# The first branch product of a token mixer in seven block products, kept PSUM banks, and a later quarter of the modulation

## The chip, the cores and the metric

The kernel runs on one core of a Trainium2 chip. TensorE (PE in the views) multiplies, VectorE (DVE) and ScalarE (ACT) work on tiles, GpSimd (POOL) here mostly issues transfers from DRAM to DRAM and writes zeros, and SyncE (SP) issues most loads. Every engine runs its own instructions in order and waits on semaphores for the others; transfers go through 16 DMA engines. The metric is the device time of one execution in microseconds, the median of several.

## The reference

One layer of a diffusion backbone on 512 tokens of width 1024. What matters here, cut from the reference:

```python
z = h @ w_in
u, vs, q, r, ga, gb, k, v, lr = _split(z, IN_SPLITS)
a = _spatial_gating(gelu(u), gelu(vs), ...)
o, s_f, s_b = _gla_bidir(...)
ob = o.astype(h.dtype) * jax.nn.silu(r)
merged = jax.nn.sigmoid(ga) * (a @ w_br_a) + jax.nn.sigmoid(gb) * (ob @ w_br_b)
return merged @ w_o, s_f, s_b
...
x = x + g1x * y_x
hx2 = _modulate(_rms_norm(x, norm2_g[l]), sh2x, sc2x)
x = x + g2x * _conv_ffn(hx2, rows, w_up, conv_w, conv_b, w_down)
```

`r`, `ga`, `gb`, `a`, `ob` and `merged` are 512 x 1024, the three weights behind them 1024 x 1024. `g1`, `sh2`, `sc2` and `g2` are quarters of `silu(c) @ w_ada + b_ada`.

## The kernel before

Each float32 operand is split into a rounded part and a rest (`wh` and `wl` for weights, `ah` and `al` and the like for activations), and a product is three matmuls: high by high, high by low, low by high. A matmul takes 128 x 128 stationary values and 512 columns.

**The weight stream.** `specs` lists all weight blocks in the order of their use, 512 KB each. `stream_load` lets SyncE load a block into one of four `raw` buffers; `stream_split` makes `wh` by a ScalarE cast (L245) and `wl` by a VectorE subtraction (L246), in one of five buffers each; `weights()` hands out the next block and moves the stream on.

**Seven products.** r, ga and gb are computed by `gate` (L1333 is its matmul): the 2 x 2 blocks of a product take seven block products instead of eight, a11, p1, s2, a21, s3, q4 and a22. Each is 24 matmuls into a pair of PSUM banks (two weight blocks, two row halves). Three pairs are used, X, Z and Y; some products go on adding to a bank, some outputs are put together by `taken` (a ScalarE copy out of a bank, L1316) and `combine` (a VectorE sum, L1321). The sums of weight quarters that it needs are built in DRAM: `sums_build` copies a quarter into a `sum` tile and adds others to it by accumulating transfers on POOL's queue. `gate_sums` is a generator that the code moves on one step at a time, in `weights()` from position SUMS0 on and in `hook`; each transfer is tied to the instruction written before it. The sums of activations (`hx_sums`) are made once.

**r.** `r_gate` takes a sigmoid, multiplies by the normalised `o` (L1300) and then by r (L1302). `ob_turn` transposes the result (L1309) and spills it to DRAM.

**The branches.** a @ w_br_a and ob @ w_br_b and merged @ w_o are done by `wide_tm` (L398): eight blocks of weights, 192 matmuls: first four output tiles side by side, then four one after another. The tiles of `a` and `ob` lie in DRAM and are brought back by `restores`, eight tiles each, split by ScalarE and VectorE (L372, L373). `sga` and `sgb` are the gates' sigmoids; the results are multiplied in.

**The modulation.** `ada2` is background work, a step for each `tick`: a load of 256 KB (`wa`), and a VectorE multiply and add (L1194) a few steps later (ADA2); at its end the sum is split and two small matmuls with ones (L1204, L1205) bring it to all rows. Before, g1, sh and sc, and g2 all run from r to w_o, by the numbers in `ticks` and in the steps of the branches. Behind it comes the up projection, with one pair of feature blocks after another (48 matmuls each), a convolution on VectorE, and `prep`, which makes operands of down; then down, by 7 block products again.

The order of the instructions of one engine comes from a scheduler, which works on the order in the code, and from `in_order`, which fixes a piece of it.

## Time and profile before

| | us |
|---|---|
| median of 3 runs | 916.73 (916.11 to 918.77) |
| the profiled execution | 916.65 |
| its span | 914.9 |
| TensorE, VectorE, ScalarE busy | 899.8, 706.9, 449.6 |
| r gate, on TensorE | from 300.9 |
| ga, gb | from 339, from 379.3 |
| a @ w_br_a | 420.2 to 463.7 |
| ob @ w_br_b, merged @ w_o | from 463.7, from 512.3 |
| up, down | 572.9 to 801.4, from 801.4 |

The span runs from the first to the last instruction that the profiler recorded; the device time has a little around it. Times in the views are counted from the span's start. TensorE's clock was full (0.998 of it). The views quoted below give busy time and mean duration of groups of instructions, the chain of waits that ended last, and the busy time of each engine in stretches of time.

### The profile page before, as it was taken

To read this page: it belongs to the slowest core of one execution; us is meant where nothing else is said; L and a number is where in the kernel's file an instruction comes from. 1 tells how busy PE (TensorE), PEld (TensorE's weight loads), DVE (VectorE), ACT (ScalarE), POOL (GpSimd) and SP (SyncE) were. 2 spreads that over 40 slices of the span, in tenths; PEclk is the share of its full clock that TensorE was granted. 3 is DMA by queue.
4 is the path that set the end of the run, shared out by engine and by line. 5 is a ranking of instruction groups with operands and counts; after the bars stand their busy time and mean duration, and the time that the engine had idled before them with its cause. 6 is when DMAs were issued, how large, how long until landed. Compare 5 with 4: busy or idle time off the path is not lost.

```text
span 914.9 us, 12458 instructions
## 1 busy us (share of the span) xinstructions
PE 899.8 (98%) x4500; PEld 750.1 (82%) x4500; DVE 706.9 (77%) x1183; ACT 449.6 (49%) x741; POOL 86.3 (9%) x138
## 2 busy tenths in 40 slices
PE   7999999999999999999999999999999999999996
PEld 5678888888888888888888889888888888888885
DVE  6468687779776698569797657898777778998956
ACT  6256455647543556755241537443333433467643
POOL 1310112122121100000000000011111000000000
PEclk9999999999999999999999999999999999999999
DMA  9970758698799759789877660788998632355552
GB/s 285 331 251 24 237 156 162 221 293 167 200 238 253 245 190 304 243 257 401 292 284 253 235 230 25 242 209 166 210 186 200 143 92 95 118 172 191 164 159 92
DMA packets 149819, 187.99 MB, mean 205 GB/s; under 512 B 8777, under 2 KB 85909, under 8 KB 149757
## 3 DMA queue, kind: packets, MB, share of 16 engines
q1 hardware_dynamic: 127981, 133.45, 45.5%
q0 software_dynamic: 19936, 50.56, 23.5%
q10 hardware_dynamic: 1840, 3.18, 0.9%
q8 instruction: 35, 0.57, 0.2%
q14 instruction: 27, 0.22, 0.1%
HBM read 178.77 MB, written 54.53 MB: 255 GB/s over the span
## 4 chain that ended last, share of the span: by engine, by line
PE 92%; DMA 2%; DVE 2%; ACT 1%; SPq 1%; issue 0%; ACTq 0%; DVEq 0%
PE mm L380 32%; PE mm L398 19%; PE mm L1333 9%; PE gl L1716 9%; PE gl L1333 4%; PE gl L910 3%; PE gl L398 2%; PE mm L674 2%; PE mm L1716 1%; PE mm L1072 1%; PE gl L674 1%; PE mm L1022 1%; DMA raw<-in_w_in_dram 1%; DMA wa<-in_w_ada_dram 1%; PE gl L945 1%; PE gl L1229 1%
## 5 line engine op out<-in xcount | busy, mean ns | idle before, releaser
L245 ACT CAST wh<-raw 128x1024 fp32r<-128x1024 f32 x172 | 180.3, 1053 | 216.7 <-PE mm L380 87.1
L246 DVE TENSOR_TENSOR wl<-raw,wh 128x1024 fp32r<-128x1024 f32 x172 | 208.8, 1220 | 78.9 <-ACT wh L245 75.9
L380 PE MATMUL mm<-h2l,wh 128*128 128x512 f32 (+1 forms) x344 | 133.0, 387 | 0.0
L380 PE MATMUL mm<-h2h,wh 128*128 128x512 f32 (+1 forms) x344 | 133.0, 387 | 0.0
L380 PE MATMUL mm<-h2h,wl 128*128 128x512 f32 (+1 forms) x344 | 133.0, 387 | 0.0
L1563 DVE SCALAR_TENSOR_TENSOR cacc<-ca,ccol,cacc 128x441 f32<-128x441 f32 (+2 forms) x176 | 121.8, 695 | 4.1
L380 PEld LDWEIGHTS mm<-h2h,wl 128*128 128x128 f32 x344 | 64.6, 188 | 13.2
L380 PEld LDWEIGHTS mm<-h2l,wh 128*128 128x128 f32 x344 | 64.6, 188 | 13.1
L380 PEld LDWEIGHTS mm<-h2h,wh 128*128 128x128 f32 x344 | 64.6, 188 | 12.9
L1194 DVE SCALAR_TENSOR_TENSOR acc<-wa,cs,acc 128x512 f32<-128x512 f32 x64 | 46.1, 746 | 4.6 <-DMA wa<-in_w_ada_dram 4.6
L1716 PE MATMUL gl<-wh,dah 128*128 128x512 f32 x120 | 46.7, 389 | 0.0
L1716 PE MATMUL gl<-wl,dah 128*128 128x512 f32 x120 | 46.7, 389 | 0.0
L1716 PE MATMUL gl<-wh,dal 128*128 128x512 f32 x120 | 46.7, 389 | 0.0
L380 PE MATMUL mm<-hxh,wh 128*128 128x512 f32 x104 | 41.3, 397 | 0.0
L380 PE MATMUL mm<-hxl,wh 128*128 128x512 f32 x104 | 40.6, 390 | 0.0
L380 PE MATMUL mm<-hxh,wl 128*128 128x512 f32 x104 | 40.5, 390 | 0.0
L1564 ACT ACTIVATE cacc<-cacc 128x512 f32<-128x512 f32 x22 | 13.9, 632 | 49.4 <-DVE cacc L1563 49.3
L398 PE MATMUL mm<-wh,hxh 128*128 128x512 f32 x88 | 34.9, 396 | 0.9 <-ACT kq L1037 0.9
L398 PE MATMUL mm<-wl,hxh 128*128 128x512 f32 x88 | 34.3, 390 | 0.0
L398 PE MATMUL mm<-wh,hxl 128*128 128x512 f32 x88 | 34.3, 390 | 0.0
L1333 PE MATMUL gl<-wh,xs 128*128 128x512 f32 x96 | 30.8, 392 | 0.0
L1333 PE MATMUL mm<-wh,xs 128*128 128x512 f32 x96 | 30.6, 390 | 0.0
(474 smaller groups left out, 2011.8 us busy)
## 6 DMA issues: line engine op xcount, KB each, us to landing
wa<-in_w_ada_dram SPq DMA_DIRECT2D x96, 256.0 KB, 5.7
raw<-in_w_in_dram SPq DMA_DIRECT2D x46, 512.0 KB, 4.5
raw<-sum SPq DMA_DIRECT2D x44, 512.0 KB, 3.7
raw<-in_ffn_w_up_dram SPq DMA_DIRECT2D x44, 512.0 KB, 5.1
sum<-in_w_in_dram POOLq DMA_DIRECT2D x36, 512.0 KB, 6.9
sum<-in_ffn_w_down_dram POOLq DMA_DIRECT2D x30, 512.0 KB, 6.7
sum<-sum POOLq DMA_DIRECT2D x22, 512.0 KB, 7.7
raw<-in_ffn_w_down_dram SPq DMA_DIRECT2D x17, 512.0 KB, 4.2
```

Of the source, the lines that this page charges most:

```text
L245: A.copy(wh, raw)
L246: V.tensor_tensor(wl, raw, wh.bitcast(F32), op=ALU.subtract)
L380: T.matmul(ps, a[:, k, :], b[:, c0:c0 + n], start=(k == 0 and i == 0), stop=(k == KT - 1 and i == 2))
L398: T.matmul(ps, a[:, t * P:(t + 1) * P], b[:, k % 2, :], start=(k == 0 and i == 0), stop=(k == KT - 1 and i == 2))
L674: T.matmul(fps[i], a, b, start=(k == 0 and z == 0), stop=(k == KT - 1 and z == 2))
L910: T.matmul(ps, p_, q_, start=(start and z == 0), stop=(stop and z == 2))
L945: T.matmul(sc[:, i * P:(i + 1) * P], S_["k"][d][:, i, :], S_["q"][d][:, i, :], start=True, stop=True)
L1194: V.scalar_tensor_tensor(acc[i], coming.pop(0), cs[:, k, 0:1], acc[i], op0=ALU.mult, op1=ALU.add)
L1333: T.matmul(banks[t], a(kk, t), w[:, kk, :], start=(first and b == 0 and kk == 0 and i == 0), stop=(b == 1 and kk == 1 and i == 2), skip_gr ...
L1563: V.scalar_tensor_tensor(o, a_[:, r0 + dy:r1 + dy, c0 + dx:c1 + dx], wcol(tap), o, op0=ALU.mult, op1=ALU.add)
L1564: A.activation(acc, acc, AF.Gelu)
L1716: T.matmul(ps, a, w[:, kk, c0:c0 + n_], start=(first and kk == 0 and i == 0), stop=(last and kk == 1 and i == 2), skip_group_check=True)
```

## The change

In words: a @ w_br_a is computed by `gate` too, so `a` comes back from DRAM in quarters (16 loads of 128 KB) and `a_prep` makes its block sums and splits during gb. w_br_a's blocks come as 14 in the stream, after those of gb, and its eight sums are built in DRAM like the gates' (16 more transfers), with more steps of `gate_sums` in two loops further ahead. r takes one Silu on ScalarE in place of a sigmoid and a multiply. The three pairs of banks are allocated once and kept over r, ga, gb and the new gate, X and Y changing places; from the second gate on, the first product is copied by ScalarE from its bank into the bank of a21, which adds to it. The steps of `ada2` are dealt out anew: fewer in gb, g2 not before the fifth feature block of up, with its loads 12 steps ahead; sh and sc have theirs 6 ahead. In down two groups are put behind others.

```diff
 EARLY = 8
-SUMS0 = 78
+SUMS0 = 84
 ADA2 = 3
+SHSC = 6
+WT = (1, 1)
+RAW = 4
...
     R_AT = len(specs)
-    for w_ in (w_br_a, w_br_b, w_o):
+    for w_ in (w_br_b, w_o):
         for hf in range(2):
...
     gate_weights = [(quarters(wi, c0), sum_tiles(2)) for c0 in (O_R, O_GA, O_GB)]
+    gate_weights.append((quarters(w_br_a[0], 0), sum_tiles(2)))
     down_specs, specs = specs, []
...
         prod_k(kps, k1, hx, k, 0, S)
+        if k % 2:
+            next(building[1][1])
     kxs[1] = heap([P, S], s="kq")
...
         hooked[0] += 1
-        if (hooked[0] % 2 or pos[2] < 10) and 2 < pos[2] < R_AT:
+        if hooked[0] % 2 and 2 < pos[2] < R_AT:
             next(building[1][1], None)
...
                          stop=(k == KT - 1 and i == 2))
+            if k % 2:
+                next(building[1][1])
         v_out(4 + t, ps)
...
-    def ada2(*kinds):
+    def ada2(*kinds, ahead=ADA2):
         todo = [(kind, j) for kind in kinds for j in range(2)]
...
         coming, steps_ = [], [(k, i) for k in range(KT) for i in range(len(todo))]
-        for n in range(len(steps_) + ADA2):
+        for n in range(len(steps_) + ahead):
             if n < len(steps_):
...
                 coming.append(w_)
-            if n >= ADA2:
-                k, i = steps_[n - ADA2]
+            if n >= ahead:
+                k, i = steps_[n - ahead]
                 V.scalar_tensor_tensor(acc[i], coming.pop(0), cs[:, k, 0:1], acc[i], op0=ALU.mult, op1=ALU.add)
...
-    def r_sum(name):
-        for b in range(2):
-            yield [lambda kk, t, z=z: z[:, kk, t * P:(t + 1) * P] for z in hx_sums[name, b]]
-
-    def r_quad(i, hf):
+    def of_sums(found):
+        return lambda name: ([lambda kk, t, z=z: z[:, kk, t * P:(t + 1) * P] for z in found(name, b)] for b in range(2))
+
+    def r_quad(name):
+        i, hf = int(name[1]) - 1, int(name[2]) - 1
         for b in range(2):
...
-    def r_gate(hf, t, src):
+    r_sum = of_sums(lambda name, b: hx_sums[name, b])
+
+    def r_silu(src):
         z = late([P, 512], s="obt")
-        A.activation(z, src, AF.Sigmoid)
+        A.activation(z, src, AF.Silu)
+        return z
+
+    def r_gate(hf, t, z):
         for hh in range(2):
...
                                    op0=ALU.mult, op1=ALU.mult)
-        V.tensor_tensor(z, src, z, op=ALU.mult)
         ob_t[hf, t] = z
...
-    def gate(out, pool, at={}, mids=late):
-
-        X, Z, Y = ([bank() for _ in range(2)] for bank in (mm, gl, mm))
+    banks = []
+
+    def gate(out, pool, at={}, mids=late, quad=r_quad, sum_=r_sum):
+
+        fresh = not banks
+        banks.extend([bank() for _ in range(2)] for bank in (mm, gl, mm) if fresh)
+        X, Z, Y = banks
+        banks.reverse()
         later = lambda i: at.get(i, lambda: None)()
-        gate_product(X, r_quad(0, 0), True)
-        m1 = [taken(z, mids) for z in X]
+        gate_product(X, quad("a11"), True)
+        if fresh:
+            m1 = [taken(z, mids) for z in X]
+        else:
+            for t in range(2):
+                A.copy(Y[t], X[t])
         later(0)
-        gate_product(Z, r_sum("p1"), True)
+        gate_product(Z, sum_("p1"), True)
         m5 = [taken(z, mids) for z in Z]
         later(1)
-        gate_product(X, r_sum("s2"))
+        gate_product(X, sum_("s2"))
         u2 = [taken(z, mids) for z in X]
         later(2)
-        gate_product(Y, r_quad(1, 0), True)
+        gate_product(Y, quad("a21"), fresh)
         for t in range(2):
-            out(0, t, combine(Y[t], m1[t], ALU.add, pool))
+            out(0, t, combine(Y[t], m1[t], ALU.add, pool) if fresh else Y[t])
         later(3)
-        gate_product(X, r_sum("s3"))
+        gate_product(X, sum_("s3"))
         for t in range(2):
...
         later(4)
-        gate_product(Z, r_sum("q4"))
+        gate_product(Z, sum_("q4"))
         for t in range(2):
...
         later(5)
-        gate_product(X, r_quad(1, 1))
+        gate_product(X, quad("a22"))
         later(6)
...
     def r_out(hf, t, src):
+        z = r_silu(src)
         if (hf, t) in ((0, 0), (0, 1), (1, 2), (1, 3)):
-            r_gate(hf, t, src)
+            r_gate(hf, t, z)
         else:
-            pending.append((hf, t, src))
-
-    bg += [ada2("g1"), ada2("sh", "sc"), ada2("g2")]
-    ticks = [0] * 2 + [1] * 6 + [0] * 10 + [1] * 10 + [1, 2] * 7
+            pending.append((hf, t, z))
+
+    bg += [ada2("g1"), ada2("sh", "sc", ahead=SHSC)]
+    ticks = [0] * 2 + [1] * 6 + [0] * 6 + [0, 0] + [1] * 12 + [0, 1] * 7 + [1, 1, 2] * 5
     gate(r_out, heap, mids=heap)
...
         def out(hf, t, src):
-            z = src if hf or t < 2 else heap([P, 512], s=name)
+            z = src if hf else heap([P, 512], s=name)
             A.activation(z, src, AF.Sigmoid)
...
     gate(squash(sga, "sga"), heap, {i: lambda i=i: ga_step(i) for i in range(7)}, heap)
-    a_act, a_step = restores(a_kept, "a")
+    found = {}
+
+    def a_prep():
+        tiles = {}
+        for i, hf in ((0, 0), (0, 1), (1, 1), (1, 0)):
+            for b in range(2):
+                t_ = heap([P, 2, 256], s="aq")
+                for kk in range(2):
+                    dma(t_[:, kk], a_kept[4 * b + 2 * i + kk][:, hf * 256:(hf + 1) * 256])
+                tiles[f"a{i + 1}{hf + 1}", b] = t_
+            yield
+
+        def kept(name, b, src):
+            hi, lo = heap([P, 2, 256], F32R, s="ah"), late([P, 2, 256], F32R, s="al")
+            A.copy(hi, src)
+            V.tensor_tensor(lo, src, hi.bitcast(F32), op=ALU.subtract)
+            found[name, b] = hi, lo
+
+        for name in ("a11", "p1", "s2", "a21", "s3", "q4", "a22"):
+            for b in range(2):
+                a11, a12, a21, a22 = (tiles["a" + z, b] for z in ("11", "12", "21", "22"))
+                if name == "p1":
+                    p1 = tiles["p1", b] = heap([P, 2, 256], s="aq")
+                    V.tensor_tensor(p1, a12, a22, op=ALU.subtract)
+                    kept(name, b, p1)
+                elif name == "s2":
+                    p1 = tiles["p1", b]
+                    V.tensor_tensor(p1, p1, a11, op=ALU.subtract)
+                    kept(name, b, p1)
+                elif name == "s3":
+                    V.tensor_tensor(a12, a11, a12, op=ALU.subtract)
+                    kept(name, b, a12)
+                elif name == "q4":
+                    V.tensor_tensor(a21, a21, tiles["p1", b], op=ALU.add)
+                    kept(name, b, a21)
+                else:
+                    kept(name, b, tiles[name, b])
+                yield
+
+    a_steps = a_prep()
+
+    def a_step(n):
+        for _ in range(n):
+            next(a_steps, None)
+
     ob, ob_step = restores(ob_kept, "ob")
-    gate(squash(sgb_t, "sgb"), heap, {i: a_step if i > 2 else lambda i=i: ob_turn(i + 5) for i in range(7)})
-
-
-    def bra_done(hf, t, ps):
-        V.tensor_tensor(sga[hf, t], ps, sga[hf, t], op=ALU.mult)
-
-    count = [0]
-
-    def bra_step():
-        count[0] += 1
-        a_step()
-        if count[0] > 11:
+
+    def gb_step(i):
+        if i < 3:
+            ob_turn(i + 5)
+        a_step((4, 2, 2, 2, 2, 2, 2)[i])
+
+    gate(squash(sgb_t, "sgb"), heap, {i: lambda i=i: gb_step(i) for i in range(7)})
+
+    def bra_out(hf, t, src):
+        V.tensor_tensor(sga[hf, t], src, sga[hf, t], op=ALU.mult)
+
+    def bra_step(i):
+        a_step((2, 0, 0, 0, 0, 0, 0)[i])
+        if i > 3:
             ob_step()
-        tick(1 + count[0] % 2)
-
-    wide_tm(a_act, bra_done, bra_step)
+
+    a_sum = of_sums(lambda name, b: found.pop((name, b)))
+    gate(bra_out, heap, {i: lambda i=i: bra_step(i) for i in range(7)}, late, a_sum, a_sum)
     mg = []
...
         ob_step()
-        tick(2)
+        tick((1 + (len(ob) >= 8)))
...
     wide_tm(ob, brb_done, brb_step, {(2 + j // 2, 4 * (j % 2)): lambda j=j: mg_turn(j) for j in range(4)})
-    drain()
     am2 = const([P, 8], "am2")
-    V.tensor_scalar(am2, cols["sc"], 1.0, None, op0=ALU.add)
-    V.tensor_tensor(am2, am2, n2g, op=ALU.mult)
-    bm2 = cols["sh"]
+
+    def ada2_end():
+        drain()
+        V.tensor_scalar(am2, cols["sc"], 1.0, None, op0=ALU.add)
+        V.tensor_tensor(am2, am2, n2g, op=ALU.mult)
...
-    hooks += [(mg_turn, 4), (mg_turn, 5), (mg_turn, 6), (mg_turn, 7)] + [(lambda: None,)] * 4 + [(crow_turn, 0), (crow_turn, 1)]
+    hooks += [(lambda j=j: (mg_turn(j), tick(WT[0])),) for j in range(4, 8)] + [(tick, WT[1])] * 4 + [(ada2_end,)]
+    hooks += [(crow_turn, 0), (crow_turn, 1)]
     wide_tm(mg, wo_done, hook, {(2, 6): turn_first})
...
         conv_part(f, pa, pv)
+        if f == 4:
+            bg.append(ada2("g2", ahead=12))
+        last = max(i for i, z in enumerate(traced()) if z.engine == V.engine)
+        tick(4 if f < 7 else 2)
+        in_order(last, V.engine)
         prep(min(EARLY, BLOCKS, (f + 1) // 4) if f < 4 * BLOCKS - 2 else min(EARLY, f - 4 * BLOCKS + 3 + BLOCKS))
...
+    def behind_last(f, *engines):
+        ends = [max(i for i, z in enumerate(traced()) if z.engine == e.engine) for e in engines]
+        f()
+        for e, i in zip(engines, ends):
+            in_order(i, e.engine)
+
     def product_in(ps, t, c0, n_, z, first, last):
...
     def operands():
-        prep(n[0] + LEAD)
+        behind_last(lambda: prep(n[0] + LEAD), A, V)
         z = weights(), ready[n[0]]
...
         rest_in(Y[t], t, w, False)
-        left(t, combine(Y[t], m1[t], ALU.add))
+        todo.append(lambda t=t: behind_last(lambda: left(t, combine(Y[t], m1[t], ALU.add)), A, V))
     products(X, False)
```

Three places of the order. The first is TensorE, where the first branch product begins (L398 before, L1348 now; `ah` and `al` are the splits of `a`). Before:

```order
L398 MATMUL mm_4487<-wh_4441,ah_4428 128x512
L398 MATMUL mm_4487<-wl_4442,ah_4428 128x512
L398 MATMUL mm_4487<-wh_4441,al_4429 128x512
L398 MATMUL mm_4488<-wh_4441,ah_4428 128x512
L398 MATMUL mm_4488<-wl_4442,ah_4428 128x512
L398 MATMUL mm_4488<-wh_4441,al_4429 128x512
```

and now:

```order
L1348 MATMUL mm_3393<-wh_4455,ah_4219 128x512
L1348 MATMUL mm_3393<-wl_4456,ah_4219 128x512
L1348 MATMUL mm_3393<-wh_4455,al_4220 128x512
L1348 MATMUL mm_3393<-wh_4455,ah_4219 128x512
L1348 MATMUL mm_3393<-wl_4456,ah_4219 128x512
L1348 MATMUL mm_3393<-wh_4455,al_4220 128x512
L1348 MATMUL mm_3393<-wh_4504,ah_4223 128x512
L1348 MATMUL mm_3393<-wl_4505,ah_4223 128x512
```

A weight block was used by four output tiles in turn, three matmuls for each; now one bank takes all that belongs to it from one pair of blocks, 12 matmuls, before the other bank is begun, and the product has 168 matmuls, not 192.

The second is VectorE at the end of that product (names: `sga` and `dc` on L1490 are outputs times the sigmoid of ga, L1336 the sums of `combine`, `obl` the rest part of ob's tiles for the next product). Before:

```order
L1416 TENSOR_TENSOR dc_4016<-gl_4707,dc_4016 128x512
L1194 SCALAR_TENSOR_TENSOR acc_4266<-wa_1075_4733,cs,acc_4266 128x512
L1194 SCALAR_TENSOR_TENSOR acc_4269<-wa_1076_4736,cs,acc_4269 128x512
L1194 SCALAR_TENSOR_TENSOR acc_4272<-wa_1077_4739,cs,acc_4272 128x512
L1194 SCALAR_TENSOR_TENSOR acc_4275<-wa_1079_4768,cs,acc_4275 128x512
L1194 SCALAR_TENSOR_TENSOR acc_4266<-wa_1080_4771,cs,acc_4266 128x512
L1416 TENSOR_TENSOR dc_4019<-mm_4742,dc_4019 128x512
L1194 SCALAR_TENSOR_TENSOR acc_4269<-wa_1082_4776,cs,acc_4269 128x512
L373 TENSOR_TENSOR obl_4816<-ob_4774,obh_4815 128x512
L1194 SCALAR_TENSOR_TENSOR acc_4272<-wa_1085_4807,cs,acc_4272 128x512
```

and now:

```order
L250 TENSOR_TENSOR wl_4820<-raw_4770,wh_4819 128x1024
L1490 TENSOR_TENSOR dc_4028<-dc_4802,dc_4028 128x512
L1205 SCALAR_TENSOR_TENSOR acc_4510<-wa_1074_4722,cs,acc_4510 128x512
L1336 TENSOR_TENSOR dc_4805<-gl_3392,dt_4658 128x512
L1205 SCALAR_TENSOR_TENSOR acc_4513<-wa_1081_4763,cs,acc_4513 128x512
L1490 TENSOR_TENSOR dc_4031<-dc_4805,dc_4031 128x512
L250 TENSOR_TENSOR wl_4865<-raw_4814,wh_4864 128x1024
L1490 TENSOR_TENSOR sga_4090<-mm_3393,sga_4090 128x512
L377 TENSOR_TENSOR obl_4855<-ob_4755,obh_4854 128x512
L250 TENSOR_TENSOR wl_4913<-raw_4823,wh_4912 128x1024
L1490 TENSOR_TENSOR sga_4092<-mm_3394,sga_4092 128x512
L377 TENSOR_TENSOR obl_4885<-ob_4808,obh_4884 128x512
```

Before, vector steps of the modulation and splits of ob's tiles stand between the outputs; now weight splits, sums and multiplies stand ahead of the first split of ob, and the last output behind it.

The third is POOL's queue behind the last spill of `a` (`kept`), at the start of r (L214 and L216 are the plain and the accumulating transfers into `sum` tiles). Before:

```order
L1221 DMA kept_3359<-ug_3301 128x512
L1221 DMA kept_3374<-ug_3349 128x512
L1180 MEMSET acc_4266 128x512
L1180 MEMSET acc_4269 128x512
L1180 MEMSET acc_4272 128x512
L1180 MEMSET acc_4275 128x512
L1180 MEMSET acc_5011 128x512
```

and now:

```order
L1234 DMA kept_3372<-ug_3313 128x512
L1234 DMA kept_3387<-ug_3362 128x512
L216 DMA sum_159<-in_w_br_a_dram 256x512
L214 DMA sum_164<-in_w_br_a_dram 256x512
L214 DMA sum_166<-in_w_br_a_dram 256x512
L216 DMA sum_163<-in_w_br_a_dram 256x512
L216 DMA sum_160<-sum_159 256x512
L216 DMA sum_162<-in_w_br_a_dram 256x512
L216 DMA sum_161<-sum_160 256x512
L216 DMA sum_166<-in_w_br_a_dram 256x512
L216 DMA sum_164<-sum_163 256x512
L216 DMA sum_165<-sum_164 256x512
```

Two plain and eight accumulating transfers for w_br_a now stand between the spills and the zeros of the next `ada2`; the sums of down's weights come behind them in both.

More of the change, by code (lines that the diff above doesn't have):

```diff
@@ L231, in stream_load @@
             ap, kn, n = specs[i]
-            raw = wp.tile([P, kn, n], F32, tag="raw", name=nm("raw"), bufs=4)
+            raw = wp.tile([P, kn, n], F32, tag="raw", name=nm("raw"), bufs=RAW)
             dma(raw, ap)
@@ L278, in backbone_kernel @@
     fv = [tuple(wp.tile([P, 2, 512], dt, tag=tag, name=nm(tag), **kw)
-                for tag, dt, kw in (("raw", F32, dict(bufs=4)), ("wh", F32R, {}), ("wl", F32R, {})))
+                for tag, dt, kw in (("raw", F32, dict(bufs=RAW)), ("wh", F32R, {}), ("wl", F32R, {})))
           for _ in range(4)]
@@ L399, in wide_step, with wide_tm @@
                      stop=(k == KT - 1 and i == 2))
-    def wide_tm(acts, done, step, at={}):
+    def wide_tm(acts, done, step, at={}, strict=False):
         pss = [mm() for _ in range(4)]
@@ L414, in wide_tm @@
             done(0, t, pss[t])
+        start = len(traced())
         ws = [weights() for _ in range(KT // 2)]
         for t in range(4):
+            if t == 2 and strict:
+                in_order(start, T.engine)
             ps = (mm if t else gl)()
@@ L1217, in ada2 @@
             yield
+    a_kept, ob_kept = [], {}
     def spill(src, start=G.dma_start):
@@ L1222, in spill @@
         return d
-    a_kept, ob_kept = [], {}
     def sgu_part(j, ug):
@@ L1505, in norm2_out @@
             A.activation(f[:, kk * 256:(kk + 1) * 256], ps[:, kk * 256:(kk + 1) * 256], AF.Identity,
-                         bias=bm2[:, k:k + 1], scale=am2[:, k:k + 1])
+                         bias=cols["sh"][:, k:k + 1], scale=am2[:, k:k + 1])
         for kk in range(2):
```

## The prediction

> **What bounds the kernel now.** I read the page first: the span, the engines' busy time, and the shares of the chain of waits.
>
> ```profile
> span 914.9 us, 12458 instructions
> PE 899.8 (98%) x4500; PEld 750.1 (82%) x4500; DVE 706.9 (77%) x1183; ACT 449.6 (49%) x741; POOL 86.3 (9%) x138
> ...
> PE 92%; DMA 2%; DVE 2%; ACT 1%; SPq 1%; issue 0%; ACTq 0%; DVEq 0%
> ```
>
> TensorE is busy for 98% of the span and is 92% of the chain that ends last. So time goes when TensorE gets less work, and comes when something makes TensorE wait. A busy share alone does not give the price of one matmul. For that I read the chain in order of time (start, length, what), where a run of matmuls stands with its count, beside the group of the same matmuls by line.
>
> ```profile
> 300.89 5.46 PE mm L1333 x24
> ...
> 420.16 21.76 PE mm L398 x96
> 441.92 5.44 PE gl L398 x24
> 447.36 24.49 PE mm L398 x108
> ...
> 572.90 228.51 PE mm L380 x1008
> ```
> ```profile
> L398 PE MATMUL mm<-wh,ah 128*128 128x512 f32 x56 | 21.8, 389 | 0.0
> ```
>
> The group says 389 ns for one matmul, but 96 of them stand in 21.76 us and 1008 in 228.51 us: 0.2267 us each. The records overlap, one matmul starts while the one before drains. The rate, not the record, is the price. A block of 24 matmuls is 5.44 us. The stages around the change have no other time in them: a @ w_br_a is 8 such blocks (192 matmuls) from 420.16, 43.5 us; each gate before it is 7 blocks (168 matmuls).
>
> Third, the busy time of each engine by stage (PE, PEld, DVE, ACT, POOL, clock, DMA share, GB/s): the stretch to 184 us, the sgu stage, the r gate, ga, gb, a @ w_br_a, ob @ w_br_b, and the up projection.
>
> ```profile
> 150.00:184.00 34.00, 33.12 (x181) 28.40 (x179) 26.57 (x61) 20.06 (x43) 5.50 (x9) 1.00 0.71 207
> ...
> 248.00:301.00 53.00, 53.00 (x272) 45.08 (x272) 36.83 (x62) 21.58 (x33) 10.47 (x15) 1.00 0.94 241
> 301.00:339.00 38.00, 38.00 (x169) 31.48 (x168) 31.63 (x45) 21.00 (x26) 1.08 (x2) 1.00 0.66 208
> 339.00:379.30 40.30, 40.30 (x189) 33.30 (x188) 32.03 (x41) 25.14 (x34) 1.99 (x4) 1.00 0.88 289
> 379.30:420.20 40.90, 40.90 (x187) 33.61 (x186) 27.38 (x33) 26.39 (x37) 0.00 (x0) 1.00 0.84 279
> 420.20:463.70 43.50, 43.50 (x193) 36.03 (x192) 36.56 (x51) 17.12 (x25) 1.06 (x2) 1.00 0.80 295
> 463.70:512.30 48.60, 48.60 (x222) 39.99 (x222) 42.50 (x63) 15.25 (x21) 3.37 (x6) 1.00 0.72 258
> ...
> 572.90:801.40 228.50, 228.50 (x1009) 189.25 (x1009) 191.42 (x273) 89.89 (x119) 21.27 (x26) 1.00 0.68 167
> ```
>
> From 184 us to the end of up TensorE never rests; its clock is full. VectorE is the next engine (84% in a @ w_br_a, 87% behind it, 84% in up), then the transfers.
>
> **Part one, the matmuls.** a @ w_br_a goes from 192 to 168 matmuls: 24 × 0.2267 = 5.44 us less on the engine that sets the end. Nothing else on TensorE changes in number; transposes and the small products of the modulation vectors stay, some at other places. (By the records' 389 ns it would be 9.3 us, which is wrong for the reason above.)
>
> The Trainium skill, "TensorE: Matmul & The Clock Gate", section "Back-to-back issue gap", gives about 131 ns for a matmul of 512 columns in a stream with weight loads, and about 216 ns alone. By the first the saving would be 3.1 us and the time about 913.6 us, by the second 5.2 us. The trace does not agree with the first: 1008 matmuls with their weight loads ran at 227 ns each.
>
> **Part two, VectorE and ScalarE.** Durations (busy, mean ns, idle before) are from the page's groups, then from the r gate alone, then over the run of ScalarE:
>
> ```profile
> L245 ACT CAST wh<-raw 128x1024 fp32r<-128x1024 f32 x172 | 180.3, 1053 | 216.7 <-PE mm L380 87.1
> L246 DVE TENSOR_TENSOR wl<-raw,wh 128x1024 fp32r<-128x1024 f32 x172 | 208.8, 1220 | 78.9 <-ACT wh L245 75.9
> ...
> L1194 DVE SCALAR_TENSOR_TENSOR acc<-wa,cs,acc 128x512 f32<-128x512 f32 x64 | 46.1, 746 | 4.6 <-DMA wa<-in_w_ada_dram 4.6
> ```
> ```profile
> L1302 DVE TENSOR_TENSOR obt<-dc,obt 128x512 f32<-128x512 f32 x4 | 2.7, 682 | 0.0
> ```
> ```profile
> L1316 ACT COPY dt<-mm 128x512 f32<-128x512 f32 x12 | 7.1, 588 | 9.1 <-PE mm L1333 9.1
> ```
> ```profile
> L1296 ACT ACT_TABLE_LOAD x1 | 1.3, 1283 | 0.0
> ```
>
> *r by Silu*: eight multiplies (L1302, over r and ga) fall away, 8 × 0.68 = 5.5 us of VectorE; one more table load, 1.28 us of ScalarE, which has 17 of 38 us free in r. TensorE waited for neither, so both count nothing.
>
> *Seeds*: two ScalarE copies (0.59 us each) and no VectorE sum for two outputs of ga, gb and the new gate. The seeded bank is first multiplied into two products later, 10.88 us; hidden. If a seed lost that cover it would cost 0.59 us per gate.
>
> *Operands of the new gate* are made in gb: 14 splits and 8 block sums on VectorE in place of 8 splits. The tiles hold 512 elements a partition like those of L1302, so 14 × 0.68 = 9.5 us more; with 14 weight blocks and 7 vector steps of 0.75 instead of 21 (−10.5 us), two sums and two multiplies less, VectorE stays below 31 of 40.9 us. Hidden.
>
> *The new gate itself* on VectorE: 14 × 1.22 (wl) + 18 × 0.746 + (four sums and eight multiplies) × 0.68 = 38.7 us by busy time, against 7 × 5.44 = 38.1 us of TensorE. This is the tight place. The one point at which VectorE is needed is its end: ob @ w_br_b begins with the split of ob's first tile. From the first output of the new gate to that split VectorE has 6 wl, 6 vector steps and 12 of the 0.68 kind in its order: 7.32 + 4.48 + 8.21 = 20.0 us by busy time. TensorE takes 2.72 + 3 × 5.44 + 0.45 (two matmuls before the first that needs the split) = 19.5 us. By busy time 0.5 us late. But busy times overlap: the timeline of VectorE in the stretch behind 453 us shows it.
>
> ```profile
> 453.44 0.74 DVE L1194 SCALAR_TENSOR_TENSOR acc<-wa,cs,acc 128x512 f32<-128x512 f32 x1
> 454.11 0.68 DVE L373 TENSOR_TENSOR obl<-ob,obh 128x512 fp32r<-128x512 f32 x1
> 454.71 0.75 DVE L1194 SCALAR_TENSOR_TENSOR acc<-wa,cs,acc 128x512 f32<-128x512 f32 x1
> ...
> 462.47 1.22 DVE L246 TENSOR_TENSOR wl<-raw,wh 128x1024 fp32r<-128x1024 f32 x1
> 463.60 0.69 DVE L373 TENSOR_TENSOR accl<-acc,acch 128x512 fp32r<-128x512 f32 x1
> ```
>
> Starts lie 0.67, 0.60 and 1.13 us apart, so the 24 take 6 × 1.13 + 6 × 0.67 + 12 × 0.60 = 18.0 us: 1.5 us early. Bounds 0 and +1 us (0.5 us, and as much for waits inside the chain); no gain is possible, since TensorE has no idle time here to win. I take 0: starts, not records, are what an engine's order costs.
>
> *g2 in up*: 16 vector steps (12 us), two splits and four small products move from behind 463.7 us to up. The sum of TensorE stays. VectorE in up: 191.4 + 12 + 1.4 = 205 of 228.5 us. In the busiest feature blocks it is 9.1 + 2 × 0.75 = 10.6 of 10.88 us: full, but the weight splits run blocks ahead. Bounds 0 and +1 us, with no idle time to win here either; I take 0. The loads of g2 run 12 steps ahead, more than one feature block. Reorderings in down touch no number; 0.
>
> **Part three, the transfers.** w_br_a now comes as 14 blocks of 512 KB, not 8, and eight of them are sums built in DRAM by 16 more transfers on POOL's queue, eight of them accumulating. Of the whole run's queues, and of the raw loads (us to landing, in the run and then in the sgu stage alone):
>
> ```profile
> q0 software_dynamic: 19936, 50.56, 23.5%
> ...
> raw<-in_w_in_dram SPq DMA_DIRECT2D x46, 512.0 KB, 4.5
> ```
> ```profile
> raw<-in_w_in_dram SPq DMA_DIRECT2D x5, 512.0 KB, 8.7
> ```
>
> POOL's queue held the 16 engines for 0.235 × 914.9 = 215 us over 50.56 MB, 4.25 us per MB; a sum of 0.52 MB is 2.2 us, the 16 are 36 us. By the order of the change ten of them are tied to steps of the r gate: 22 us on top of 0.66 × 38 = 25 us, 47 us of work in 38 us. ga brings 35.5 us of its own into 40.3. Only in gb, where 14 vector loads go, is there room again. So from 301 to about 385 us the engines will be near full. What that does is shown by the sgu stage: share 0.94, raw loads 8.7 us instead of 4.5, TensorE 53.00 of 53.00. Four raw buffers turn over in landing + cast + wl, 8.7 + 1.05 + 1.22 = 11.0 us, against four blocks of TensorE, 10.9 us: level. Before that the stream has a lead, which a row of SyncE's timeline at the start of r shows.
>
> ```profile
> 301.29 0.37 SPq L233 DMA_DIRECT2D raw<-sum  x1
> ```
>
> This is the ninth of r's 14 blocks; it serves the fifth product, due at 300.89 + 4 × 5.44 = 322.65. From these 21.4 us go 4.5 for landing and 2.3 for cast and wl: some 15 us of lead. Cost 0; bounds 0 (no idle time to win) and the third rival.
>
> One place is already in arrears: the chain before 184 us.
>
> ```profile
> 172.84 1.22 DVE wl L246
> 174.07 8.18 DMA raw<-in_w_in_dram
> 182.32 1.05 ACT wh L245
> 183.37 0.51 ACT kq L1037
> 183.92 0.96 PE mm L398 x3
> ```
>
> TensorE misses 34.00 − 33.12 = 0.88 us here, for a raw load that took 8.18 us beside sums on POOL's queue. The change starts the sums earlier (twelve move into 63 to 97 us), and leaves accumulating ones beside this load. Bounds: −0.9 us (the load lands in 4.5) and +1 us. I take 0.
>
> **Sum.** 914.9 − 5.44 = 909.5 us span; 916.65 − 914.9 = 1.75 us lie around the span, so 911.2 us against the profiled run, and 911.3 against the median 916.73, 0.08 above it.
>
> **The rivals.**
> 1. *The arrears at 184 us go too.* For it: fewer sums are left beside the load. Against it: those left are accumulating. 910.3 us.
> 2. *VectorE takes back a part*, at the joint to ob @ w_br_b, in up, or both. For it: 20.0 against 19.5 us, 10.6 against 10.88. Against it: the starts. 1 to 3 us: 912.3 to 914.3, middle 913.3 us.
> 3. *Slower: the sums starve the raw loads in r and ga.* 28 blocks are loaded there. The lead of 15 us is gone when each block is 15 / 28 = 0.54 us late, four in 13.0 us, which is a landing of 10.8 us. The gain is eaten too at (15 + 5.4) / 28 = 0.73 us, a landing of 11.5 us. At 12.5 us four blocks take 14.8 us, each 0.97 us late, 27 − 15 = 12 us in all: 923 us. For it: 47 us of transfers in 38. Against it: 0.94 in sgu cost TensorE nothing. The Trainium skill, "DMA: Bandwidth & Descriptors", section "Queues, rings and completion order", says that each DMA engine takes turns between queues packet by packet; by that the raw loads keep their half, and this rival would fall away. The 8.18 us above are no proof of either.
> 4. *The change does not take the block's time out*, because the kept banks make each of the seven products wait for a ScalarE copy out of a bank: 7 × 0.59 = 4.1 us, so 915.3 us. Against it: the r gate, which has the same form, starts with 24 matmuls in 5.46 us at 300.89, and its stage is 38.00 of 38.00 busy.
>
> **Chances.** Forecast 0.53 (its own range 910.6 to 912.2), first rival 0.10, second 0.20, third 0.13, fourth 0.04. A measurement of this kernel cannot tell less than 0.3% (2.75 us) from no change, so faster ends at 913.98 us and slower begins at 919.48. Faster: 0.53 + 0.10 + half of the second, 0.10 = 0.73. Same: the other half, 0.10, and the fourth, 0.04 = 0.14. Slower: the third, 0.13. The range runs from just under the first rival, 909.8 us, to 917 us, past the second and fourth; about 0.12 is left out above, in the third.
>
> **What would show it.** Seven products of 5.44 us behind gb, each without idle time ahead, show part one right. At its end, an idle row of the first matmul with obl, released by a VectorE row, would be the second rival; a VectorE share above 0.97 in up with idle TensorE also. Raw loads that land in 10.8 us or more in r and ga, and matmuls waiting for wh or wl there, would be the third. The row of kq before 184 us tells the first. The forecast is wrong if TensorE's busy time falls by less than 5 us or its idle time behind 184 us rises above 1 us.

## The result, and the profile after

The changed kernel takes 920.64 us, the median of 13 executions (915.6 to 922.54), and the kernel before 916.44 us of 13 (914.9 to 918.77). The ratio is 1.0041, 95% interval 1.0028 to 1.0055: slower by 4.2 us, where 5.4 us less was forecast. The profiled execution took 921.7 us with a span of 920.0 us, so the two spans differ by 5.1 us.

First the page of the changed kernel: span, busy time, shares of the chain of waits.

```profile
span 920.0 us, 12481 instructions
...
PE 897.4 (98%) x4476; PEld 746.5 (81%) x4476; DVE 717.3 (78%) x1195; ACT 461.3 (50%) x760; POOL 97.4 (11%) x154
...
PE 86%; DMA 7%; DVE 4%; ACT 2%; issue 1%; SPq 0%; ACTq 0%; DVEq 0%
```

TensorE has 24 matmuls less, and its share of the chain fell from 92% to 86%. Transfers now hold 7% of the chain, 64 us, where they held 2%. What TensorE waited for (total, times, longest):

```profile
PE gl L945 <- DVE lc L912: 3.4, 1, 3.4
PE mm L1348 <- DVE wl L250: 2.6, 3, 1.3
PE gl L1348 <- DVE wl L250: 1.4, 1, 1.4
PE mm L1348 <- ACT wh L249: 1.0, 1, 1.0
PE mm L402 <- ACT kq L1046: 0.5, 1, 0.5
```

Only the last of these rows stood in the profile before, with 0.9. The four others are new: one wait of 3.4 us near 96 us, and 5.0 us at the gates' matmuls (L1348), for split weights. The four gates by stage (r, ga, gb, a @ w_br_a), from the first matmul of one to that of the next; the columns are the busy times of PE, PEld, DVE, ACT and POOL, then TensorE's clock, the DMA share and GB/s:

```profile
304.30:344.20 39.90, 38.62 (x172) 31.50 (x171) 25.14 (x34) 17.62 (x22) 8.56 (x11) 1.00 1.01 276
344.20:389.50 45.30, 41.55 (x188) 33.10 (x187) 32.01 (x42) 27.63 (x37) 0.88 (x1) 1.00 0.92 288
389.50:430.50 41.00, 41.00 (x188) 33.58 (x187) 29.29 (x36) 31.20 (x47) 1.91 (x4) 1.00 0.77 260
430.50:468.50 38.00, 38.00 (x169) 31.50 (x168) 36.54 (x47) 22.52 (x31) 0.00 (x0) 1.00 0.96 353
```

The last row is the predicted gain: 38.0 us where the wide product took 43.5, with TensorE busy throughout. The first two are a loss. Before, the first matmuls of r, ga and gb start at 300.65, 338.82 and 379.24 us, so r took 38.2 us and ga 40.4; now they take 39.9 and 45.3, together 6.6 us more. Of these, 5.0 us are the waits. The other 1.6 us come with the five stops, about 0.3 us each: matmuls start 0.227 us apart but their records last 0.39 to 0.50 us, and at a stop one has no other to overlap with. The DMA share is 1.01 in r, at only 276 GB/s.

The other loss is early. The chain of waits of the changed kernel from 85 us on:

```profile
85.31 9.22 DMA raw<-in_w_in_dram
...
95.56 0.73 ACT lc L842
...
96.92 0.67 DVE suf L852
97.58 0.80 DVE wl L250
...
98.62 0.69 DVE lc L912
...
99.36 1.12 PE gl L945 x4
```

A weight block lands after 9.22 us. Before, the load at this place took 3.6 us (the issues between 79 and 91 us, with the time to landing):

```profile
raw<-in_w_in_dram SPq DMA_DIRECT2D x1, 512.0 KB, 3.6
```

ScalarE shows why that stops TensorE, though no matmul uses the block before 121 us. ScalarE's timeline before, and then after:

```profile
91.27 0.63 ACT L832 ACTIVATE lc<-lc 128x512 f32<-128x512 f32 x1
91.81 1.04 ACT L245 CAST wh<-raw 128x1024 fp32r<-128x1024 f32 x1
92.75 0.72 ACT L833 ACTIVATE lc<-lc,one_t 128x512 f32<-128x512 f32 x1
```
```profile
89.30 0.63 ACT L841 ACTIVATE lc<-lc 128x512 f32<-128x512 f32 x1
94.61 1.05 ACT L249 CAST wh<-raw 128x1024 fp32r<-128x1024 f32 x1 [4.67 <-DMA raw<-in_w_in_dram]
95.56 0.72 ACT L842 ACTIVATE lc<-lc,one_t 128x512 f32<-128x512 f32 x1
```

The cast of the block stands between two steps of the decays `lc`. ScalarE works in order, so the second step waits 4.67 us behind a cast that nobody is in a hurry for, and the transposes of `lc` stop TensorE. The stop costs twice, as the stretches around it show, with the same columns:

```profile
97.00:100.00 3.00, 0.64 (x3) 0.65 (x4) 2.84 (x5) 2.44 (x5) 0.04 (x1) 0.66 0.83 261
100.00:102.00 2.00, 2.00 (x8) 1.61 (x7) 2.00 (x4) 1.26 (x3) 0.83 (x2) 0.50 1.08 291
102.00:104.00 2.00, 2.00 (x6) 1.61 (x5) 0.28 (x1) 0.00 (x0) 1.08 (x3) 0.50 0.95 351
104.00:106.00 2.00, 2.00 (x8) 1.59 (x8) 0.00 (x0) 0.00 (x0) 0.71 (x1) 0.81 1.01 324
106.00:150.00 44.00, 44.00 (x259) 38.93 (x258) 32.57 (x74) 23.05 (x52) 4.37 (x6) 1.00 0.52 125
```

The clock falls to 0.50 near 98 us, while TensorE still waits, and is back at 1.00 by 105 us; 0.66 and 0.81 are means over their stretches. So TensorE works for about five microseconds at half clock. Matched one by one, its matmuls are 2.0 us ahead of the kernel before from 50 to 96 us, and 4.0 us behind once the clock is full again. One group as an example, before and after:

```profile
104.02 1.78 PE gl L945 x16
```
```profile
108.00 1.78 PE gl L954 x16
```

That is 6.0 us lost, 3.4 by the wait and 2.6 behind it, at the low clock.

The account of the two spans: start −2.0 (in the other profiled executions below it lies between −1.8 and +0.9), early stop +6.0, the wait for kq near 184 us −0.4, r and ga +6.6, the branch product −5.4; sum +4.8 of the 5.1 us.

### The profile page after: what moved, and what is told of

It reads as the page before. It is cut to its first block, busy times and chain, and to the rows that moved or that the text cites. A ratio compares the mean times of both kernels' runs of the same rounds, so it can differ in the third digit from the quotient of the medians.

```text
span 920.0 us, 12481 instructions
## 1 busy us (share of the span) xinstructions
PE 897.4 (98%) x4476; PEld 746.5 (81%) x4476; DVE 717.3 (78%) x1195; ACT 461.3 (50%) x760; POOL 97.4 (11%) x154
## 4 chain that ended last, share of the span: by engine, by line
PE 86%; DMA 7%; DVE 4%; ACT 2%; issue 1%; SPq 0%; ACTq 0%; DVEq 0%
PE mm L384 31%; PE mm L402 15%; PE gl L1800 9%; PE mm L1348 9%; PE gl L1348 3%; PE gl L919 3%; DMA raw<-sum 3%; PE mm L681 2%; DMA raw<-in_w_in_dram 2%; PE gl L402 2%; DMA wa<-in_w_ada_dram 2%; PE mm L1800 1%; PE gl L681 1%; DVE wl L250 1%; PE gl L590 1%
## 5 line engine op out<-in xcount | busy, mean ns | idle before, releaser
L249 ACT CAST wh<-raw 128x1024 fp32r<-128x1024 f32 x178 | 186.4, 1052 | 216.7 <-PE mm L384 80.0
L250 DVE TENSOR_TENSOR wl<-raw,wh 128x1024 fp32r<-128x1024 f32 x178 | 215.7, 1219 | 63.4 <-ACT wh L249 57.9
L216 POOL DMA_DIRECT2D sum<-sum x26 | 22.9, 891 | 134.7 <-PE mm L384 43.8
L214 POOL DMA_DIRECT2D sum<-in_ffn_w_down_dram x20 | 11.6, 579 | 187.5 <-DVE wl L250 90.2
```

The costliest lines, as they stand in the source:

```text
L216: G.dma_start(sums[b][dst], ap, accum_op=ALU.add)
L249: A.copy(wh, raw)
L250: V.tensor_tensor(wl, raw, wh.bitcast(F32), op=ALU.subtract)
```

## The experiments

Two theories were set against each other. Theory S: the transfers on POOL's queue that build sums in DRAM starve the weight loads, at both places. Rival D: the new order of the work on VectorE and ScalarE makes the waits. All ratios are against runs of the kernel before on the same chip.

**Sums of w_br_a left out.** The blocks that would be sums are loaded as plain quarters, so the branch product is not that of the reference.

```diff
-    gate_weights.append((quarters(w_br_a[0], 0), sum_tiles(2)))
+    bra_quarter = quarters(w_br_a[0], 0)
+    gate_weights.append((bra_quarter, [[bra_quarter(b, 0, 0)] * 4 for b in range(2)]))
...
-        for z in gate_weights:
+        for z in gate_weights[:3]:
```

> The changed kernel without the 16 transfers that build w_br_a's sums: the blocks that would be sums are loaded as plain quarters of w_br_a (same bytes), so the branch product is not that of the reference. Theory S (the transfers on POOL's queue starve the raw loads at two places, near 85 us and in r): the r gate takes about 38 us again instead of 44.6, no raw load in r lands later than 9 us, and the stall near 97 us stays; time about 920 - 6.5 = 913 to 915 us. Rival D (the new order on VectorE and ScalarE in r, with vector steps of the modulation ahead of weight splits, makes the wait): r stays at 43 us or more, time 919 to 921 us.

916.05 us (914.44 to 917.53), ratio 0.9989 (0.9977 to 1.0002). In its stages, r and ga:

```profile
303.80:342.00 38.20, 38.20 (x171) 31.66 (x170) 31.35 (x45) 22.56 (x28) 1.08 (x2) 1.00 0.73 223
342.00:382.40 40.40, 40.40 (x188) 33.38 (x187) 27.44 (x31) 25.67 (x33) 0.00 (x0) 1.00 0.88 279
```

38.2 and 40.4 us, the lengths of before, with the new order of VectorE, Silu, seeds and vector steps all in place. The early stop stays (2.7 us of waiting for `lc`), here without a fall of the clock, which is 1.00 from 96 to 110 us. The time is 1 us above the expected window's top. D falls for r and ga. (The expectation gives all of the loss to r, 44.6 us; by the stages above 1.7 us of it are r's and 4.9 us ga's.)

**Early steps left out.**

```diff
         prod_k(kps, k1, hx, k, 0, S)
-        if k % 2:
-            next(building[1][1])
...
-            if k % 2:
-                next(building[1][1])
         v_out(4 + t, ps)
```

> The changed kernel without the 12 added steps of gate_sums in the two early loops; all sums are still built, 12 steps later each, so those of w_br_a now fall into r and ga. Theory S: no wait at 95 to 100 us and a full clock there (5.6 us won), and the wait in r as long or longer, since more accumulating transfers stand there: 914 to 919 us. Rival D: the same win early, r unchanged: 914 to 916 us. A third view, that the early loss has nothing to do with the sums: 919 to 921 us.

929.34 us (928.66 to 931.45), ratio 1.0145 (1.0130 to 1.0160), 10 us above the window that was expected. The early stop is gone; r takes 40.6 us, ga 53.0 and gb 45.8. Over the undisturbed 38.2, 40.4 and 40.8 us that is 20 us lost, 13 more than in the changed kernel, by sums that come 12 steps later. The direction is S's; neither theory gave the size.

**Both left out.**

> Both edits together: no sums of w_br_a (blocks loaded as plain quarters, so the branch product is not that of the reference) and no early steps. Theory S: both waits gone, what is left is the predicted gain of 24 matmuls, 5.4 us: 910 to 912 us. Rival D: the wait in r stays, 915 to 918 us.

911.12 us (910.62 to 913.62), ratio 0.9947 (0.9932 to 0.9963). Without the 16 transfers and the early steps the kernel does what was predicted: 911.3 us was forecast. That the two agree to 0.2 us is partly luck, since r still takes 39.5 us here, 1.3 us more than undisturbed, with four accumulating transfers of the gates' own sums in it.

**The kernel before with the early steps alone.**

```diff
         prod_k(kps, k1, hx, k, 0, S)
+        if k % 2:
+            next(building[1][1])
...
+            if k % 2:
+                next(building[1][1])
         v_out(4 + t, ps)
...
-        if (hooked[0] % 2 or pos[2] < 10) and 2 < pos[2] < R_AT:
+        if hooked[0] % 2 and 2 < pos[2] < R_AT:
```

> The kernel before with the 12 early steps of gate_sums added and the hook's early clause taken out, nothing else. Theory S: the raw load issued near 85 us lands after 9 us instead of 3.6, TensorE waits 3.4 us for lc near 96 us and runs at half clock behind it, together 5 to 6 us; part may come back where sums leave 98 to 177 us (the 0.9 us before 184 us): 920 to 922 us. Rival: the early steps alone cost nothing, 916 to 917 us.

920.81 us (920.29 to 925.13), ratio 1.0066 (1.0045 to 1.0086), as S expected: a wait of 3.9 us for `lc`, a mean clock of 0.81 from 97 to 106 us, and r, ga and gb at 38.2, 40.4 and 40.8 us. The early loss needs nothing else of the change.

**Early plain steps kept, early accumulating ones put later.**

```diff
-            if k % 2:
+            if k % 2 and t == 0:
                 next(building[1][1])
         v_out(4 + t, ps)
```

> The changed kernel with the eight early plain transfers kept and the four early accumulating ones given to later steps. Theory S in the form that accumulating transfers (8 to 15 us to land) starve the raw load issued near 85 us: the wait near 96 us goes, 5 us won there, while r gets four more steps of sums, so 917 to 922 us in all; the row of the raw load near 85 us tells. If plain ones do the same, that load still lands after 8 us or more.

920.03 us (918.63 to 921.7), ratio 1.0043 (1.0030 to 1.0056). The transfers between 79 and 91 us (queue, then issues with the time to landing), first of the changed kernel, then of this run:

```profile
q0 software_dynamic: 924, 2.11, 91.6%
...
sum<-in_w_in_dram POOLq DMA_DIRECT2D x4, 512.0 KB, 11.1
raw<-in_w_in_dram SPq DMA_DIRECT2D x3, 512.0 KB, 9.2
```
```profile
q0 software_dynamic: 360, 1.28, 32.8%
...
sum<-in_w_in_dram POOLq DMA_DIRECT2D x1, 512.0 KB, 5.9
raw<-in_w_in_dram SPq DMA_DIRECT2D x1, 512.0 KB, 3.8
```

Eight plain transfers cost nothing; the four accumulating ones that stood last were the early loss. Whether four plain ones in their place would have cost as much was not tried. Put later, they stand in r and ga, and ga grows to 50.9 us. What was won early was lost there.

**The kernel before with the early steps and the 16 transfers, unread.** This is the loss in r without any of the change's other parts but the early steps.

```diff
-        for z in gate_weights:
+        for z in gate_weights + [(quarters(w_br_a[0], 0), sum_tiles(2))]:
             yield from sums_build(*z)
```

> The kernel before with the early steps (its run alone: 920.81 us) and with the 16 transfers for w_br_a's sums issued where the change issues them; nothing reads them, the branch product is as before. Theory S: the wait in r and ga comes with these transfers alone, 5 to 7 us over the run with early steps: 925 to 928 us, the ga stage 45 us instead of 40.4. Rival D (the changed order of the other work): 920 to 922 us.

930.29 us (929.4 to 930.53), ratio 1.0155 (1.0141 to 1.0168), 9.5 us over the run with early steps alone. r takes 46.3 us instead of 38.2, ga stays at 40.4. The stage was named wrongly (ga), and the size was larger than expected; the cause is S's.

**The same with the eight accumulating transfers made plain.**

```diff
-                    if len(step) == 4:
+                    if len(step) == 4 or not add:
```

Here `add` is false for w_br_a alone.

> As the run before, with the eight accumulating transfers of w_br_a made plain copies of the same size. If it is the accumulating form that loads the engines, the wait in r and ga falls to 2 us or less: 920 to 923 us. If it is the number or the bytes of transfers, it stays: 925 to 928 us.

922.84 us (922.39 to 923.49), ratio 1.0076 (1.0062 to 1.0089). First r of the run before, then of this one, and for each POOL's queue between 300 and 350 us:

```profile
305.90:352.20 46.30, 41.34 (x170) 33.35 (x170) 31.16 (x42) 20.19 (x26) 9.01 (x12) 0.93 1.01 280
```
```profile
q0 software_dynamic: 2686, 6.37, 55.5%
```
```profile
305.40:344.60 39.20, 38.48 (x171) 31.55 (x171) 30.59 (x42) 20.57 (x26) 6.64 (x12) 1.00 0.90 316
```
```profile
q0 software_dynamic: 1885, 6.73, 37.6%
```

With as many transfers and slightly more bytes, r loses 1.0 us instead of 8.1. Plain, the queue held the engines 0.376 × 50 = 18.8 us for 6.73 MB, 2.8 us per MB; with accumulating ones 27.8 us for 6.37 MB, 4.4 us per MB. The accumulating form is what loads the engines. (The rest of the 2.0 us over the run with early steps alone lies ahead of r: r starts 1.1 us later.)

**No vector steps in r.** In the changed kernel the chain through r alternates between late weight blocks and late blocks of the modulation:

```profile
311.54 9.65 DMA wa<-in_w_ada_dram
...
323.20 11.96 DMA raw<-sum
...
337.60 11.57 DMA raw<-sum
...
352.34 6.48 DMA wa<-in_w_ada_dram
...
358.84 1.41 DVE acc L1205 x2
360.26 1.15 DVE wl L250
```

A vector step waits for its load and holds up the weight split behind it. This run moves six such steps from r to gb.

```diff
-    ticks = [0] * 2 + [1] * 6 + [0] * 6 + [0, 0] + [1] * 12 + [0, 1] * 7 + [1, 1, 2] * 5
+    ticks = [0] * 14 + [0, 0] + [1] * 12 + [1] * 13 + [0] + [1, 1, 2] * 5
```

> The changed kernel with the six modulation steps of r moved to gb, sums untouched. It tells whether the wait in r comes through VectorE's multiply and add that stands ahead of a weight split and waits for its own 256 KB load (11.1 us of such waits in r), or through the raw loads themselves. Through VectorE: r falls from 44.6 to 40 us or less, time 914 to 917 us. Through the raw loads (landings of 12 us): r stays above 42 us, 918 to 921 us; six loads less are 1.6 MB of the 13.4 MB that r moves, 12%.

922.78 us (918.76 to 926.16), ratio 1.0070 (1.0044 to 1.0096). r takes 38.2 us again and ga loses 2.3 us, where the two lost 6.6, but gb and the branch product are 1.1 and 2.1 us longer than undisturbed: 5.5 us in all. VectorE's waits for blocks of w_ada fell from 11.1 to 1.2 us in r and the start of ga; 3.0 us of waiting for the modulation's bias (`acc` from b_ada) are new. So part of the sums' harm goes through these steps, but taking the loads away from r mostly moved the wait; neither expectation held as a whole. The median says less: the four executions spread over 7 us, and the profiled one, 925.09 us, also waits 2.1 us for kq ahead of r.

**The sums dealt out anew.** The changed kernel's DMA share from 104 to 187 us is 0.50. This version keeps the eight plain early steps and puts the others into the six value tiles there (`v_units`).

```diff
-            if k % 2:
+            if k % 2 and t == 0:
                 next(building[1][1])
         v_out(4 + t, ps)
...
             hook()
             hook()
+            for _ in range(3):
+                next(building[1][1])
```

> The whole change, with the 64 sum transfers dealt out anew: of the 12 early steps only the eight plain ones stay, and each of the six value tiles between 104 and 187 us, where the DMA share of the changed kernel is about 0.5, gets three steps more; w_br_a's sums are then all built before r. Theory S: full clock and no wait near 96 us, r at 38 us, 911 to 913 us, faster than both kernels, unless the wait near 184 us (0.9 us before) grows with the transfers now there. Rival D (order on VectorE in r): 915 us or more.

910.09 us (908.83 to 911.2), ratio 0.9931 (0.9919 to 0.9943), with the whole computation: faster than both kernels. Its stages from r to the branch product, and the stretch that took the sums:

```profile
298.20:336.40 38.20, 38.20 (x172) 31.64 (x170) 34.75 (x50) 24.56 (x31) 2.63 (x5) 1.00 0.81 256
336.40:376.80 40.40, 40.40 (x189) 33.39 (x188) 27.49 (x31) 25.72 (x33) 0.00 (x0) 1.00 0.86 279
376.80:417.60 40.80, 40.80 (x188) 33.58 (x187) 31.07 (x40) 32.52 (x49) 1.92 (x4) 1.00 0.78 246
417.60:455.70 38.10, 38.10 (x170) 31.55 (x169) 34.29 (x43) 21.00 (x27) 0.00 (x0) 1.00 0.98 344
104.00:187.00 83.00, 83.00 (x477) 72.96 (x477) 62.13 (x139) 47.31 (x103) 16.11 (x21) 1.00 0.85 198
```

TensorE is busy in all of it. The sums went where the share was 0.50 and made it 0.85 at no cost. The wait for kq near 184 us is gone as well.

**Two steps more in the value tiles instead of three.**

> As the run before, with two steps more for each value tile instead of three: a few accumulating sums of w_br_a are left at the start of r. Theory S: between 911 and 914 us; better than the run before only if its wait near 184 us is the larger part.

915.44 us (911.49 to 917.79), ratio 0.9983 (0.9969 to 0.9998), above the expected window. Its twelve executions spread over 6 us. The profiled one took 911.71 us and loses 0.9 us in r; what the longer ones wait for was not recorded and stays open.

**Silu and seeds undone**, on the version dealt out anew: r's sigmoid and multiply, and the copies and sums of the a21 outputs, are back.

```diff
-        A.activation(z, src, AF.Silu)
+        A.activation(z, src, AF.Sigmoid)
+        V.tensor_tensor(z, src, z, op=ALU.mult)
...
-            for t in range(2):
-                A.copy(Y[t], X[t])
+        m1 = [taken(z, mids) for z in X]
...
-            out(0, t, combine(Y[t], m1[t], ALU.add, pool) if fresh else Y[t])
+            out(0, t, combine(Y[t], m1[t], ALU.add, pool))
```

> The re-dealt version (sums in the value tiles) with two parts of the change undone: r's sigmoid and VectorE multiply are back, and the a21 outputs are put together by a ScalarE copy and a VectorE sum again. The prediction priced both parts at nothing, hidden behind TensorE: then 909.5 to 911 us, as the re-dealt version with its 910.09. Rival: VectorE is what limits the gates; 8 multiplies and 6 sums, 14 x 0.68 = 9.5 us, come back in part: 912 us or more.

910.70 us (909.21 to 911.87), ratio 0.9940 (0.9926 to 0.9953), against 0.9931 (0.9919 to 0.9943) with them: the intervals overlap. The medians differ by 0.6 us, or by 1.0 us when each is taken against the kernel before on its own chip. In its profiled execution, at 911.87 us the longest of five, r took 40.6 us instead of 38.2, with 1.6 us of waiting for `wl`.

## Why the prediction was wrong, step by step

**The matmuls: right.** The branch product took 38.0 us instead of 43.5. Where the transfers do not disturb, the median falls by 5.0 us (both edits left out) and by 6.1 us (sums dealt out anew). The rate of the chain, 227 ns a matmul, was the right price, not the 389 ns of a record. The Trainium skill's page "TensorE: Matmul & The Clock Gate", section "Back-to-back issue gap", has 131 ns, by which the gain is an estimated 3.1 us; the measurement decides.

**VectorE and ScalarE: right as far as tried.** Silu and seeds together are worth 1 us at most by the medians, and nothing within the noise. At the joint to ob @ w_br_b, where 20.0 us by busy time stood against 19.5, the changed kernel shows no wait, which agrees with the starts. g2 moved 0.9 us of small products into up, 229.4 us instead of 228.5, and the stretch from ob @ w_br_b to up is 1.1 us shorter.

**The transfers: wrong, twice.** The step that failed is "Cost 0" for the 16 sums in r and ga, and with it the twelve early steps, which had no price but that of the load before 184 us.

First, the twelve early steps were weighed only by what they leave beside the load before 184 us, with bounds of −0.9 and +1 us; that wait did fall, by 0.4 us. The place that they moved *to* was not worked out: what loads stand there, and what stands behind these loads on ScalarE. It cost 6.0 us. The half clock behind a stop was in no term. There, beside the accumulating transfers, the two queues from 85.3 to 94.5 us were:

```profile
q0 software_dynamic: 751, 1.46, 87.7%
q1 hardware_dynamic: 333, 0.65, 21.3%
```

The weight loads (q1) got about a fifth of the engines' time while one to four of them were under way. The rule on turns between queues in the Trainium skill's page "DMA: Bandwidth & Descriptors", section "Queues, rings and completion order", has the queues take turns packet by packet, and the prediction had read that as a half for them. 333 packets beside 751 are not equal turns, if the profile's packets are those that the Trainium skill means, which no run shows; as to the share, the measurement decides.

Second, the sums in r. Their price by the mean over POOL's queue, 4.25 us per MB, was right: 4.4 was measured. What failed is the step from the sgu stage to r: a share of 0.94 and a landing of 8.7 us cost TensorE nothing there, so they were taken to cost nothing in r. But TensorE uses 8 weight blocks in the 53 us of sgu and 14 in the 38 us of r. POOL's queue held the same share of the engines in both, in sgu of the kernel before (248 to 301 us) and in r and the start of ga of the changed one (304 to 352 us):

```profile
q0 software_dynamic: 2461, 5.39, 52.8%
```
```profile
q0 software_dynamic: 2451, 5.52, 53.0%
```

By this count a late block has time in sgu and none in r, though no run varied it. And in r the loads landed later than the 8.7 us at which the four buffers were level: after 11.7 us in the median for blocks of w_in, and two of the sums after 11.57 and 11.96 us.

The third rival named this mechanism, the landings (11.57 and 11.96 us, where 10.8 was its threshold) and r and ga as its place. It had a chance of only 0.13, and it knew neither the early stop nor the way through the vector steps. The lead of 15 us was used up and 6.6 us lost beyond it; with that alone the time would have been about 1 us over the kernel before, and the early 6.0 us did the rest, less what the start of the profiled execution won.

**The range** ended at 917 us because the third rival, 923 us, was left above it on the strength of sgu's 0.94. The measured 920.64 us is not that rival's sum either: it gave 12 us to r and ga, where 6.6 were lost, and nothing to the early site. Two sites of the same mechanism added up to a time near its own, which is luck.

## What to carry to other kernels

A transfer that is moved has to be priced where it goes: which loads share the engines there, and which instruction stands in order behind the one that needs the load. A cast that nobody hurries for can stop the engine that sets the end, if a step of the critical chain comes after it in the queue. Before adding accumulating transfers, look for a stretch with a low DMA share; here the same transfers, dealt out over other instructions, made about 10 us of difference (920.64 and 910.09 us).

## What was not expected of the hardware

A stop of TensorE of 3.4 us brought a clock of 0.50 from about 98 to 104.5 us, 2.6 us of extra time. In all five profiled executions with a stop of 3.4 to 3.9 us at this place the clock fell to 0.50; in the one with a stop of 2.7 us, without w_br_a's sums, it stayed at 1.00. Four accumulating transfers of 512 KB from DRAM to DRAM landed after 11.1 us in the median, a plain one just ahead of that place after 5.9; the queue's engine time was 4.4 us per MB with accumulating ones in it and 2.8 us with plain ones alone. A share of 1.01 can go with 276 GB/s, in r, and a share of 0.98 with 344 GB/s.
